# A two-layer diffusion backbone on one core: the products of V as one step per head, the order searched in ten stretches, and a pad of 32 bytes

## The chip, the cores and the metric

The kernel runs on one core of a Trainium2 chip. The core has a matrix engine, TensorE (PE in the rows; its weight loads stand apart as PEld), and three engines for everything that is not a matrix product: VectorE (DVE), ScalarE (ACT) and GpSimd (POOL). SyncE (SP) issues the transfers between HBM and the on-chip memory SBUF. TensorE writes its results into PSUM, eight banks of 128 x 512 numbers. The metric is the device time of one execution in microseconds; the times of a kernel are given as the median of three runs.

## The reference: what is computed

512 latent tokens `x` and 256 context tokens `ctx`, each of 1024 features, pass two layers. Each layer is a token mixer and a squared-ReLU MLP, both behind an RMS norm and a modulation (shift, scale, gate) made from a conditioning vector. Layer 0 mixes by neighbourhood attention with 16 heads of 64 features; layer 1 mixes by sliding-window attention with 4 heads of K and V for 16 of Q, a sink logit and rotary positions. Latent queries attend in one softmax to their local latent keys and to all context keys. Only layer 0 computes new context tokens. Cut to what matters:

```python
for i in range(DEPTH):                       # DEPTH = 2
    u_lat = modulate(rms_norm(h_lat, g_mix[i]), sh1, sc1)
    u_ctx = modulate(rms_norm(h_ctx, g_mix[i]), csh1, csc1)
    if i % 2 == 0:
        q, k, v = split(u @ na_wqkv)         # latent and context, q and k normed
        y_lat = neighborhood_attention(ql, kl, vl, kc, vc, na_rpb) @ na_wo
        y_ctx = context_attention(qc, kc, vc) @ na_wo
    else:
        y_lat = sliding_window_attention(rope(ql), rope(kl), vl, kc, vc, swa_sink) @ swa_wo
    h_lat = h_lat + ga1 * y_lat
    h_lat = h_lat + ga2 * (square(relu(modulate(rms_norm(h_lat)) @ mlp_w1[i])) @ mlp_w2[i])
    # layer 0 does the same for h_ctx with y_ctx
# one head and one block of queries:
s = concat(q @ k_local.T * scale + bias, q @ k_ctx.T * scale)
p = softmax(s)
o = p[local] @ v_local + p[ctx] @ v_ctx
```

All of it is in 32-bit floats.

## The kernel before, in words

**Products.** The large products (projections, scores, MLP) take each operand as a sum of two rounded parts (type fp32r), so one product is three on TensorE. The transposes of the attention weights and the products of V take plain 32-bit floats. One such product is one instruction of the program, and the trace shows it as two rows.

**Attention of a head.** `attn0(p, i)` is one head of layer 0, `Head1` one of layer 1. The scores of four blocks of 128 latent queries (and, in layer 0, of the context queries) come out of TensorE, VectorE adds bias or mask, ScalarE takes the exponential, and the result is scaled. TensorE then transposes these weights piece by piece into PSUM banks of the pool `p_pt`. `evac_pt` copies four (or three) transposed blocks at a time from PSUM into one slot of `PTr`, on ScalarE or VectorE. These slots lie in the region tile R.

**The products of V.** V of a head has 64 columns, half the width of TensorE. `mm_halves` issues two products that use the left and the right half (`tile_position` (0, 0) and (0, 64)) and write to the upper and the lower half of one PSUM bank, `po`. In the rows of the trace these products are called `128*64`. Layer 0 has four such steps for each head: the two blocks of context keys (512 columns each), two pairs of local blocks (192 and 256 columns), and last the context's own queries (256 columns). Layer 1 has three: 512, 256 and 384 columns. `merge` then adds the two halves of the bank: one copy of one half into `otmp` and one add on VectorE.

**What sets the order.** The code records every operation as a `Step` with its reads and writes; `together()` makes one step of several instructions of TensorE. A planner (`Plan`) then gives each step a cost by a table of its own and decides, engine by engine, which step stands next. The order of an engine is fixed by this before the kernel runs. Some steps may go to either of two engines, and the planner chooses. `Plan.search` tries many orders: it starts from the order of the code, moves steps that TensorE waited for forward (`hurry`), shakes the ranking by random amounts (`shaken`) and keeps the best. It does so in two stretches. The first ends at `cut`, in the middle of the MLP of layer 0; the second takes the rest. Since every operation is issued by one line of `build`, nearly all rows of the trace have the same line, L542, and are told apart by their tiles.

**Memory.** RA (rounded parts) and FA (floats) are two large tiles, then come small constants (`ident`, the identity for the transposes, `perm`, `ones`, `cst` and others), and behind them the region tile R, which is used for four things in turn: a ring of loads, V and `PTr` in layer 0, weights in the MLPs, and V and `PTr` again in layer 1. The eight PSUM banks are called pq.

**Stages.** By the profile: loading and the first norms from 0 to 40 us, the first projections up to 80 us, attention of layer 0 from 80 to 425 us with the projections of the next heads woven in, its output projection up to 470 us, the MLP of layer 0 up to 1000 us, keys and values of layer 1 up to 1082 us, its attention up to 1225 us, and the rest up to 1617.7 us.

Of the kernel before, what the change touches and what calls it, by code (L numbers as in the profile page):

```python
# [118 lines left out]
class Plan:  # L119
# [98 lines left out]
    def cost(self, x):  # L218
        if x.eng == "PE":
# [16 lines left out]
            else:  # L236
# [7 lines left out]
                x.occ = sum(2 * (m / 1.2 + (47 if cols == 64 else 3)) for m in runs)  # L244
# [219 lines left out]
    def search(self, rounds, tries, cut):  # L464
# [7 lines left out]
        rnd = random.Random(1)  # L472

        def of(rank, first, upto):
            s = self.forward(rank, first.copy(), upto)
            s.rank, s.last = rank, s.start[cut] if upto else max(s.end)
            return s

        def rounds_of(rank, first, upto, n, least=200):
            best = None  # L480
            for k in range(n):
# [3 lines left out]
                rank = self.hurry(rank if s.last < best.last * 1.004 else best.rank, s, least)  # L485
            return best

        first, rank = self.begin(), [float(x.i) for x in self.steps]
        for upto in (cut, None):
            found = [rounds_of(rank, first, upto, 3 * rounds)]  # L490
            for k in range(tries):
                found.sort(key=lambda s: s.last)
                found.append(rounds_of(self.shaken(found[k % 2].rank, rnd), first, upto, rounds, rnd.choice((100, 200))))
            first = best = min(found, key=lambda s: s.last)
        s = best
# [24 lines left out]
def build(nc, tc, a):  # L520

    with ExitStack() as es:
        plan, regions, cut = _build(nc, tc, a, es)
# [12 lines left out]
        for step in plan.search(ROUNDS, TRIES, cut):  # L536
# [9 lines left out]
ROUNDS, TRIES = 10, 24  # L546
# [9 lines left out]
def _build(nc, tc, a, es):  # L556
# [76 lines left out]

    (RX,) = region((F32, 4096))
# [297 lines left out]
    def bias_tables():  # L932

        for c in range(16):
# [3 lines left out]
            yield  # L938

# [171 lines left out]
    def attn0(p, i):  # L1111
# [61 lines left out]
        mm_halves(blocks, start=True)  # L1173
# [7 lines left out]
        mm_halves([(po[:, 0:192], Vs(0), pt[:, 0:192]), (po[:, 64:320], Vs(1), pt[:, 192:448])])  # L1181
# [7 lines left out]
        mm_halves([(po[:, 192:448], Vs(2), pt[:, 0:256]), (po[:, 320:512], Vs(3), pt[:, 256:448])], stop=True)  # L1189
        merge(OT_lat[:, p], po, i)  # L1190
# [208 lines left out]
    for p in range(7):  # L1399
# [5 lines left out]
        else:  # L1405
            run(ad)
            p_mm = Banks(4, 5)
            weave(at, (qkv0(p + 1), 7))
# [581 lines left out]
```

## Time and profile before

| what | before |
|---|---|
| median of 3 runs | 1621.09 us (1620.41 to 1621.33) |
| the profiled execution | 1619.86 us |
| its span (first to last instruction) | 1617.7 us |
| instructions in the span | 24693 |
| TensorE busy | 1596.9 us, 99% |
| VectorE, ScalarE, GpSimd busy | 1174.1, 814.0, 248.3 us |
| granted clock of TensorE, mean | 0.999 |

Times in the rows below are microseconds from the start of the span, unless a column says otherwise. A row of the timeline gives the start, the length, the engine, the operation, what it writes and reads, its shape, and how many instructions of the kind follow each other (x4); in brackets stands how long the engine was idle before it, and what ended the wait. Successive products overlap in the array, so the length of a row runs past the start of the next one: the time that a row takes from its engine is read from start to start. Some records of products are missing in a trace, so a count in such a row can be a little low.

### The profile page before, as it was taken

What the parts mean: (1) busy time and instruction counts of PE and PEld (TensorE: products, weight loads), DVE (VectorE), ACT (ScalarE), POOL (GpSimd) and SP (SyncE); (2) the same over time, 40 slices, a digit from 0 to 9 for tenths busy, and PEclk for the clock granted to TensorE, in tenths of its full rate; (3) what the DMA queues carried; (4) which work ended last, traced back from release to release, by engine and by line L of the source; (5) the groups of instructions that cost most, each with busy time, mean ns of one, the idle gap of its engine ahead of it and who ended that gap; (6) DMA issues with size and microseconds to landing.
All of it is one profiled execution on the core that took longest, in us unless ns stands there. A gap on an engine that the chain in (4) does not pass through costs nothing.

```text
span 1617.7 us, 24693 instructions
## 1 busy us (share of the span) xinstructions
PE 1596.9 (99%) x9356; PEld 1332.1 (82%) x9356; DVE 1174.1 (73%) x2376; ACT 814.0 (50%) x1627; POOL 248.3 (15%) x220
## 2 busy tenths in 40 slices
PE   8999999999999999999999999999999999999999
PEld 4788888887888888888888888787768888888887
DVE  4798777887488676676786767999996855556554
ACT  4687667776355242434442523677894533222220
POOL 0111111111123020312230211342200000000000
PEclk9999999999999999999999999999999999999999
DMA  9643343123324232333341422010024332222301
GB/s 347 198 134 98 116 128 99 49 65 118 102 78 147 91 129 92 119 117 129 120 141 54 142 92 78 24 43 27 20 73 163 105 105 91 102 94 79 104 27 52
DMA packets 57400, 165.59 MB, mean 102 GB/s; under 512 B 6593, under 2 KB 16193, under 8 KB 57153
## 3 DMA queue, kind: packets, MB, share of 16 engines
q1 hardware_dynamic: 57280, 164.01, 31.0%
q8 instruction: 73, 1.20, 0.3%
q14 instruction: 47, 0.38, 0.1%
HBM read 159.79 MB, written 7.34 MB: 103 GB/s over the span
## 4 chain that ended last, share of the span: by engine, by line
PE 92%; DVE 5%; ACT 2%; issue 1%; DMA 1%; POOL 0%; SPq 0%; DVEq 0%; ACTq 0%; POOLq 0%
PE pq L542 92%; DVE FA L542 2%; DVE RA L542 2%; DVE smalls L542 1%; ACT FA L542 1%; ACT RA L542 0%; ACT R L542 0%; DMA FA<-in_wqkv_dram 0%; DMA FA<-in_xT_dram 0%; POOL FA L542 0%; ACT smalls L542 0%; DVE R L542 0%; SPq L542 0%; DVEq L542 0%; DVE amod L542 0%
## 5 line engine op out<-in xcount | busy, mean ns | idle before, releaser
L542 PE MATMUL pq<-RA 128*128 128x512 f32 (+3 forms) x6560 | 1274.6, 348 | 6.9 <-ACT RA L542 2.8
L542 PEld LDWEIGHTS pq<-RA 128*128 128x128 f32 x6560 | 1053.5, 189 | 166.5 <-issue 14.5
L542 ACT CAST RA<-FA 128x1024 fp32r<-128x1024 f32 (+3 forms) x283 | 225.9, 812 | 347.6 <-PE pq L542 260.8
L542 DVE SCALAR_TENSOR_TENSOR FA<-pq,mods,FA 128x512 f32<-128x512 f32 (+1 forms) x413 | 263.5, 661 | 132.9 <-PE pq L542 131.6
L542 DVE TENSOR_TENSOR RA<-FA,RA 128x1024 fp32r<-128x1024 f32 (+3 forms) x248 | 244.4, 997 | 98.1 <-ACT RA L542 96.7
L542 PE MATMUL pq<-RA,R 128*128 128x512 f32 (+1 forms) x870 | 182.3, 352 | 0.0
L542 PEld LDWEIGHTS pq<-RA,R 128*128 128x128 f32 x870 | 143.7, 188 | 25.4 <-issue 0.8
L542 ACT ACTIVATE FA<-FA,smalls 128x512 f32<-128x512 f32 (+1 forms) x166 | 121.4, 741 | 26.8 <-DVE smalls L542 26.2
L542 POOL TENSOR_TENSOR RA<-FA,RA 128x512 fp32r<-128x512 f32 (+1 forms) x35 | 51.0, 1457 | 539.8 <-ACT RA L542 539.2
L542 PE MATMUL pq<-ident,FA 128*128 128x128 f32 x800 | 129.8, 276 | 3.2 <-DVE FA L542 1.9
L542 PEld LDWEIGHTS pq<-ident,FA 128*128 128x128 f32 x800 | 94.8, 140 | 26.4 <-issue 6.9
L542 DVE TENSOR_TENSOR R<-R,FA 128x1024 f32<-128x1024 f32 x84 | 103.8, 1260 | 15.0 <-ACT FA L542 7.8
L542 POOL TENSOR_SCALAR FA<-FA,s 128x1024 f32<-128x1024 f32 x24 | 78.4, 3265 | 221.7 <-DMA FA<-in_ada_w_dram 179.0
L542 POOL TENSOR_TENSOR FA<-FA,smalls 128x256 f32<-128x256 f32 (+2 forms) x81 | 59.8, 743 | 341.4 <-DVE smalls L542 249.3
L542 ACT ACTIVATE FA<-FA,s 128x1024 f32<-128x1024 f32 x60 | 68.9, 1151 | 69.5 <-POOL FA L542 54.0
L542 ACT ACTIVATE FA<-pq 128x512 f32<-128x512 f32 (+1 forms) x96 | 49.9, 522 | 82.6 <-PE pq L542 82.6
L542 DVE SCALAR_TENSOR_TENSOR FA<-pq,FA 128x512 f32<-128x512 f32 (+1 forms) x96 | 57.0, 596 | 45.4 <-ACT FA L542 45.2
L542 ACT ACTIVATE FA<-FA 128x256 f32<-128x256 f32 (+1 forms) x130 | 58.9, 455 | 47.7 <-DVE FA L542 42.7
L542 ACT COPY R<-pq 128x512 f32<-128x512 f32 (+4 forms) x145 | 68.6, 491 | 28.2 <-PE pq L542 25.7
L542 PE MATMUL pq<-R 128*64 128x512 f32 (+2 forms) x448 | 79.2, 463 | 0.7 <-DVE FA L542 0.7
L542 POOL TENSOR_TENSOR FA<-FA 128x256 f32<-128x256 f32 (+2 forms) x59 | 47.4, 816 | 191.5 <-ACT FA L542 130.5
L542 ACT COPY FA<-pq 128x256 f32<-128x256 f32 (+4 forms) x98 | 42.4, 433 | 57.1 <-PE pq L542 54.2
(84 smaller groups left out, 994.7 us busy)
## 6 DMA issues: line engine op xcount, KB each, us to landing
FA<-in_w_dram SPq DMA_DIRECT2D x128, 512.0 KB, 3.5
FA<-in_ada_w_dram SPq DMA_DIRECT2D x80, 512.0 KB, 3.8
FA<-in_wqkv_dram SPq DMA_DIRECT2D x24, 384.0 KB, 3.3
FA<-in_wo_dram SPq DMA_DIRECT2D x16, 512.0 KB, 3.4
FA<-in_ada_dram SPq DMA_DIRECT2D x10, 512.0 KB, 10.3
FA<-in_wq_dram SPq DMA_DIRECT2D x8, 512.0 KB, 3.5
R<-in_ada_dram SPq DMA_DIRECT2D x6, 512.0 KB, 10.9
FA<-in_xT_dram SPq DMA_DIRECT2D x4, 512.0 KB, 6.7
```

Of the source, the lines that this page charges most:

```text
L542: tc.keep_in_program_order(getattr(e, f)(*map(real, args), **{k: real(x) for k, x in kw.items()}))
```

## The change

Three things are changed, and two smaller ones go with them.

First, `mm_halves` takes all products of V of a head at once and makes one step of them. In layer 0 that joins the four steps of a head (the product for the context's queries included, which now writes to a bank of `p_pt` instead of the bank of V), in layer 1 the three steps. The planner's cost for such a step is adapted by one term.

Second, `search` takes a list of marks instead of the one `cut`. There are ten marks: after the heads p = 0, 2, 4 and 6 of layer 0, after the output projection, in the middle of the MLP, after the keys and values of layer 1, and after each of the first three groups of heads of layer 1. Each stretch is searched with a look ahead to the next mark, by the time that TensorE spends without work; the numbers of rounds and tries are 8 and 16 instead of 10 and 24.

Third, a constant of 128 x 8 floats (32 bytes in each partition) is placed between FA and the constants, so that the region tile begins at a multiple of 128 bytes.

In layer 1 `PTr` has five slots instead of three, one of them in FA; for this the mask is cut from 896 to 640 columns, and the rotary tables move.

```diff
-                x.occ = sum(2 * (m / 1.2 + (47 if cols == 64 else 3)) for m in runs)
+                x.occ = sum(2 * (m / 1.2 + (47 if cols == 64 else 3)) for m in runs) - (38 * (len(runs) - 1) if cols == 64 else 0)
...
-            s.rank, s.last = rank, s.start[cut] if upto else max(s.end)
+            s.rank, s.last = rank, (max(s.free[pe], s.start[upto]) if upto else max(s.end)) - s.done
...
-                rank = self.hurry(rank if s.last < best.last * 1.004 else best.rank, s, least)
+                rank = self.hurry(rank if s.last < best.last + 4000 else best.rank, s, least)
...
-        first, rank = self.begin(), [float(x.i) for x in self.steps]
-        for upto in (cut, None):
-            found = [rounds_of(rank, first, upto, 3 * rounds)]
+        source = [float(x.i) for x in self.steps]
+        first, rank, marks = self.begin(), source, cuts + [None]
+        for q, mark in enumerate(marks):
+            far = marks[min(q + 1, len(marks) - 1)]
+            found = [rounds_of(r, first, far, 2 * rounds) for r in ((rank, source) if q else (source,))]
             for k in range(tries):
                 found.sort(key=lambda s: s.last)
-                found.append(rounds_of(self.shaken(found[k % 2].rank, rnd), first, upto, rounds, rnd.choice((100, 200))))
-            first = best = min(found, key=lambda s: s.last)
+                found.append(rounds_of(self.shaken(found[k % 2].rank, rnd), first, far, rounds, rnd.choice((100, 200))))
+            best = min(found, key=lambda s: s.last)
+            rank = best.rank
+            if mark:
+                first = of(rank, first, mark)
...
-ROUNDS, TRIES = 10, 24
+ROUNDS, TRIES = 8, 16
...
+    const("pad", [128, 8])
     (RX,) = region((F32, 4096))
...
-    def mm_halves(pairs, start=False, stop=False):
+    def mm_halves(*sums):
 
         with together():
-            for at, (out, st, mv) in zip((0, 64), pairs):
-                pe.matmul(out[at : at + 64], st, mv, start=start, stop=stop, tile_position=(0, at))
+            for pairs in sums:
+                for n, pair in enumerate(pairs):
+                    for at, (out, st, mv) in zip((0, 64), pair):
+                        pe.matmul(out[at : at + 64], st, mv, start=n == 0, stop=n == len(pairs) - 1, tile_position=(0, at))
...
-        mm_halves(blocks, start=True)
+        pairs = [blocks]
...
-        mm_halves([(po[:, 0:192], Vs(0), pt[:, 0:192]), (po[:, 64:320], Vs(1), pt[:, 192:448])])
+        pairs.append([(po[:, 0:192], Vs(0), pt[:, 0:192]), (po[:, 64:320], Vs(1), pt[:, 192:448])])
...
-        mm_halves([(po[:, 192:448], Vs(2), pt[:, 0:256]), (po[:, 320:512], Vs(3), pt[:, 256:448])], stop=True)
-        merge(OT_lat[:, p], po, i)
+        pairs.append([(po[:, 192:448], Vs(2), pt[:, 0:256]), (po[:, 320:512], Vs(3), pt[:, 256:448])])
...
-        po = p_pv.next()[:, 0:256]
-        mm_halves([(po, Vs(4 + c), pt[:, c * 256 : c * 256 + 256]) for c in range(2)], start=True, stop=True)
-        merge(OT_ctx[:, p], po, i)
+        pc = p_pt.next()[:, 0:256]
+
+        mm_halves(pairs, [[(pc, Vs(4 + c), pt[:, c * 256 : c * 256 + 256]) for c in range(2)]])
+        merge(OT_lat[:, p], po, i)
+        merge(OT_ctx[:, p], pc, i)
...
-    mask = FA[:, 4096:4992]
-    rope = FA[:, 4992:6016].rearrange("p (e t d) -> p e t d", e=4, t=4)
+    mask = FA[:, 4096:4736]
+    rope = FA[:, 5120:6144].rearrange("p (e t d) -> p e t d", e=4, t=4)
...
-    PTr = Slots(*(RX[:, 2176 + 512 * i : 2688 + 512 * i] for i in range(3)))
+    PTr = Slots(*(RX[:, 2176 + 512 * i : 2688 + 512 * i] for i in range(3)), RX[:, 3712:4096], FA[:, 4736:5120])
...
             ee = ends()
-            mm_halves(blocks, start=True)
             yield
-            blocks = [mid(1)]
-            mm_halves(ee)
+            mids = [mid(1)]
             yield
-            blocks.append(mid(2))
-            yield
-            mm_halves(blocks, stop=True)
+            mids.append(mid(2))
+            mm_halves([blocks, ee, mids])
             merge(OT_lat[:, h // 2], po, h % 2)
```

The order of the instructions shows what becomes of the steps. The first place is TensorE at the last heads of layer 0. In these rows pq7 is the bank of V, R00 the region tile, `ident` the identity, and 64x512 a product of V of 512 columns. Before:

```order
L542 MATMUL pq7_72<-R00_124 64x256 x2
L542 MATMUL pq2_67<-ident_73,FA_64 128x128
L542 MATMUL pq3_68<-ident_73,FA_64 128x128 x3
L542 MATMUL pq2_67<-ident_73,FA_64 128x128
L542 MATMUL pq5_70<-RA_63 128x512 x5
L542 MATMUL pq2_67<-ident_73,FA_64 128x128 x2
L542 MATMUL pq7_72<-R00_124 64x512 x2
L542 MATMUL pq7_72<-R00_124 64x192
L542 MATMUL pq7_72<-R00_124 64x256 x2
L542 MATMUL pq7_72<-R00_124 64x192
L542 MATMUL pq4_69<-RA_63 128x512 x2
L542 MATMUL pq5_70<-RA_63 128x512
```

Here the three latent steps of a head already stand behind each other, while the context's product (the row at the top, of the head before) stands alone. In the order of the change, the same stage:

```order
L547 MATMUL pq2_68<-ident_74,FA_64 128x128 x7
L547 MATMUL pq7_73<-R00_125 64x512 x2
L547 MATMUL pq7_73<-R00_125 64x192
L547 MATMUL pq7_73<-R00_125 64x256 x2
L547 MATMUL pq7_73<-R00_125 64x192
L547 MATMUL pq6_72<-R00_125 64x256 x2
L547 MATMUL pq0_66<-RA_63 128x256 x4
L547 MATMUL pq1_67<-RA_63 128x512 x2
```

The context's product has moved up to the end of the latent ones and writes to pq6, a bank of `p_pt`. The second place is TensorE at a head in the middle of the attention of layer 1, before:

```order
L542 MATMUL pq3_68<-ident_73,FA_64 128x128
L542 MATMUL pq7_72<-R20_8853 64x512 x2
L542 MATMUL pq2_67<-RA_63 128x128 x2
L542 MATMUL pq1_66<-RA_63 128x512
L542 MATMUL pq0_65<-RA_63 128x512 x2
L542 MATMUL pq1_66<-RA_63 128x512
L542 MATMUL pq7_72<-R20_8853 64x256 x2
L542 MATMUL pq3_68<-ident_73,FA_64 128x128 x4
L542 MATMUL pq7_72<-R20_8853 64x384 x2
```

and in the order of the change, at a late head of the same layer:

```order
L547 MATMUL pq6_72<-ident_74,FA_64 128x128 x3
L547 MATMUL pq0_66<-RA_63 128x512 x6
L547 MATMUL pq4_70<-RA_63 128x512
L547 MATMUL pq7_73<-R20_8852 64x512 x2
L547 MATMUL pq7_73<-R20_8852 64x256 x2
L547 MATMUL pq7_73<-R20_8852 64x384
L547 MATMUL pq7_73<-FA_64,R20_8852 64x384
L547 MATMUL pq4_70<-RA_63 128x512 x2
```

Scores (RA, 128x512) and transposes no longer stand between the three pieces; the last piece reads its slot from FA.

## Rows read from the trace of the kernel before

**Rows 1.** The page: busy time of the engines, and the chain that ended last.

```profile
PE 1596.9 (99%) x9356; PEld 1332.1 (82%) x9356; DVE 1174.1 (73%) x2376; ACT 814.0 (50%) x1627; POOL 248.3 (15%) x220
...
PE 92%; DVE 5%; ACT 2%; issue 1%; DMA 1%; POOL 0%; SPq 0%; DVEq 0%; ACTq 0%; POOLq 0%
```

**Rows 2.** Windows: length, busy PE, PEld, DVE, ACT, POOL, granted clock, DMA share, GB/s.

```profile
80.00:425.00 345.00, 342.30 (x2284) 290.61 (x2285) 272.73 (x804) 244.63 (x648) 48.86 (x65) 1.00 0.32 101
...
1082.00:1225.00 143.00, 141.90 (x907) 100.81 (x906) 129.88 (x368) 126.33 (x283) 24.16 (x31) 1.00 0.16 54
```

**Rows 3.** Waits of PE: us in total, times, longest; of seven rows.

```profile
PE pq L542 <- DVE R L542: 5.9, 1, 5.9
...
PE pq L542 <- ACT RA L542: 2.8, 3, 1.8
...
PE pq L542 <- DVE smalls L542: 0.5, 2, 0.3
```

**Rows 4.** Timeline of PE at the longest waits behind the loading phase.

```profile
80.75 4.10 PE L542 MATMUL pq<-RA 128*128 128x256 f32 x28 [1.55 <-ACT FA L542]
...
1028.63 7.08 PE L542 MATMUL pq<-RA 128*128 128x512 f32 x28 [0.92 <-DVE RA L542]
1036.80 0.66 PE L542 MATMUL pq<-ident,FA 128*128 128x128 f32 x4 [1.09 <-DVE FA L542]
```

**Rows 5.** Timeline of PE: the first and the last of 69 groups.

```profile
91.70 1.84 PE L542 MATMUL pq<-R 128*64 128x512 f32 x12
...
1222.85 0.87 PE L542 MATMUL pq<-R 128*64 128x384 f32 x4
```

**Rows 6.** Timeline of PE, layer 1, a joined group and the next.

```profile
1094.37 1.51 PE L542 MATMUL pq<-R 128*64 128x512 f32 x8
1095.81 0.88 PE L542 MATMUL pq<-ident,FA 128*128 128x128 f32 x6
1096.62 0.87 PE L542 MATMUL pq<-R 128*64 128x384 f32 x4
1097.41 0.77 PE L542 MATMUL pq<-ident,FA 128*128 128x128 f32 x5
```

**Rows 7.** Timeline of PE, layer 1, a head whose steps stand apart.

```profile
1174.18 1.08 PE L542 MATMUL pq<-R 128*64 128x512 f32 x4
1175.19 1.41 PE L542 MATMUL pq<-RA 128*128 128x128 f32 x6
1176.53 0.65 PE L542 MATMUL pq<-R 128*64 128x256 f32 x4
1177.11 0.66 PE L542 MATMUL pq<-ident,FA 128*128 128x128 f32 x4
```

**Rows 8.** Timeline of PE: undisturbed products and transposes.

```profile
453.43 2.32 PE L542 MATMUL pq<-RA 128*128 128x256 f32 x18
455.59 0.86 PE L542 MATMUL pq<-RA,R 128*128 128x256 f32 x6
...
1196.06 1.15 PE L542 MATMUL pq<-ident,FA 128*128 128x128 f32 x9
```

**Rows 9.** Timeline of PE, layer 0, the last heads.

```profile
407.93 1.81 PE L542 MATMUL pq<-RA 128*128 128x256 f32 x13
409.67 1.84 PE L542 MATMUL pq<-R 128*64 128x512 f32 x12
411.44 7.08 PE L542 MATMUL pq<-RA 128*128 128x256 f32 x46
```

**Rows 10.** Groups by form: count, busy us, mean ns of one, idle before.

```profile
L542 PE MATMUL pq<-ident,FA 128*128 128x128 f32 x800 | 129.8, 276 | 3.2 <-DVE FA L542 1.9 <-ACT R L542 0.8 <-DVE RA L542 0.3
L542 ACT COPY R<-pq 128x512 f32<-128x512 f32 x74 | 41.7, 587 | 15.3 <-PE pq L542 14.4
L542 DVE COPY R<-pq 128x512 f32<-128x512 f32 x22 | 15.1, 687 | 6.6 <-PE pq L542 6.5
L542 PE MATMUL pq<-ident,R 128*128 128x128 f32 x40 | 10.4, 277 | 0.0
```

More of the change, by code (lines that the diff above doesn't have):

```diff
@@ L462, in shaken, with search @@
         return [r + shift.setdefault(i // size, rnd.gauss(0.0, span)) for i, r in enumerate(rank)]
-    def search(self, rounds, tries, cut):
+    def search(self, rounds, tries, cuts):
         self.epochs()
@@ L471, in search @@
                 self.steps[j].succ.append(x.i)
-        rnd = random.Random(1)
+        rnd, pe = random.Random(1), self.ALL.index("PE")
         def of(rank, first, upto):
             s = self.forward(rank, first.copy(), upto)
-            s.rank, s.last = rank, s.start[cut] if upto else max(s.end)
+            s.rank, s.last = rank, (max(s.free[pe], s.start[upto]) if upto else max(s.end)) - s.done
             return s
@@ L522, in build @@
     with ExitStack() as es:
-        plan, regions, cut = _build(nc, tc, a, es)
+        plan, regions, cuts = _build(nc, tc, a, es)
         tiles, now, open_ = {}, -1, ExitStack()
@@ L534, in turn @@
                 tiles[k, j] = pool.tile([128, n], dtype, name=f"R{k}{j}", tag="R")
-        for step in plan.search(ROUNDS, TRIES, cut):
+        for step in plan.search(ROUNDS, TRIES, cuts):
             while step.epoch is not None and now < step.epoch:
@@ L938, in bias_tables, with mark @@
             yield
+    cuts = []
+    def mark():
+        cuts.append(next(x.i for x in reversed(plan.steps) if x.eng == "PE"))
     raw, raw0 = Ring(FA, FX, 768, 2), Ring(FA, FX, 1024, 2)
@@ L1408, in _build @@
             weave(at, (qkv0(p + 1), 7))
+        if p in (0, 2, 4, 6):
+            mark()
     wo0.take(0, Stream(Ring(FA, FX, 1024, 2), [(a["wo0"][0, q], u) for q, u in enumerate((wx, wslots[2], wslots[0], wslots[3]))], 4))
@@ L1417, in _build @@
     split_o(7)
-    cut = []
     def mlp(layer, T_ctx, stream, tmp, side, st_lat, st_ctx, between=None, after_ctx=None):
@@ L1545, in mlp @@
             if c == NCH // 2 and T_ctx:
-                cut.append(next(x.i for x in reversed(plan.steps) if x.eng == "PE"))
+                mark()
             if c + 1 < NCH:
@@ L1597, in _build @@
     wo0.rest(stream, Banks(0,1,7,2,3), *st, lambda: mod_lat(0, 1, tmp2))
+    mark()
     def between():
@@ L1795, in front @@
                     scores(ps, T1, T2, q0, with_context(K, 0))
-                    mk = mask[:, 0:768].rearrange("p (s n) -> p s n", s=2)[:, :, 0:256]
+                    mk = FA[:, 4096:4864].rearrange("p (s n) -> p s n", s=2)[:, :, 0:256]
                     col[t] = {0: 256, 1: 384, 4: 0, 5: 128}
@@ L1874, in _build @@
     kv1()
+    mark()
     heads = [Head1(h) for h in range(16)]
@@ L1896, in _build @@
             weave((go(), 24 if gr else 21), (q1(gr + 1), 8))
+            mark()
         else:
@@ L1919, in _build @@
     mlp(1, False, stream, Ring(FA, FX + 5120, 512, 5), iter(()), None, None, between=lambda: half_done(256))
-    return plan, regions, cut[0]
+    return plan, regions, cuts
 def layout(inputs):
```

## The prediction, written before the changed kernel was run

> **What bounds the kernel now.** I read the page first. TensorE (PE) is busy 99% of the span of 1617.7 us, and the chain that ended last lies on it for 92% [rows 1]. The reader is to see that work taken off another engine gains nothing: time comes only from what TensorE itself spends. A busy PE is not a PE at its pace, though, so I went on to the stages. In the attention of layer 0 (80 to 425 us) and of layer 1 (1082 to 1225 us) PE is busy 342.30 of 345 and 141.90 of 143 us, at a granted clock of 1.00, the upper of its two levels (2.4 GHz) [rows 2]. The list of what PE waited for gives the real holes: seven rows that sum to 16.5 us, 5.9 us of them the first product's wait for its first input, and 1.8 us the longest of three waits for ScalarE's first results [rows 3]. The largest of the others are 1.55 us where the attention of layer 0 begins and 0.92 and 1.09 us at the hand-over between the layers [rows 4]. So waiting that another order could fill is about 16.5 - 5.9 - 1.8 = 8.8 us; whatever else can be won is hidden inside "busy".
>
> It is hidden where TensorE changes between products of full width and the products of V, which are 64 wide (128*64 in the rows). A group of 64-wide products is one row of TensorE's timeline. Between the first at 91.70 us and the last at 1222.85 us there are 69 of them, 34 in layer 0 and 35 in layer 1 [rows 5]; the order of the program before has the same 69.
>
> **What a group costs beyond its columns.** The old order already puts some of a head's steps back to back, which gives a price without an experiment. Inside: in layer 1 a joined group (512 columns, then 256; 8 rows of the trace) takes from its start to the start of what follows 1095.81 - 1094.37 = 1.44 us [rows 6]; the same two pieces apart take 1175.19 - 1174.18 = 1.01 and 1177.11 - 1176.53 = 0.58 us [rows 7]. Joining them saves 1.59 - 1.44 = 0.15 us. Outside: between two groups stand six transposes that take 1096.62 - 1095.81 = 0.81 us [rows 6]. A row of nine transposes lasts 1.15 us; less the 0.28 us that one of them lasts [rows 10], that is 0.87 us for eight steps, 0.11 us each [rows 8]. Six should take 0.66, so the change out of 64 wide and back in costs 0.15 us. Between full-width products: 13 of 256 columns stand between two groups and take 409.67 - 407.93 = 1.74 us [rows 9]; at a pace of (455.59 - 453.43) / 18 = 0.120 us [rows 8] they should take 1.56, so there the change costs 0.18 us. A group that is joined to another thus saves 0.15 + 0.15 = 0.30 us where transposes stand behind it, and 0.15 + 0.18 = 0.33 us where full-width products do.
>
> The rows give this change a price, 0.30 to 0.33 us, and not its cause. The Trainium skill has one: "Changing tiling mode (not just tile) drains the TensorE" (TensorEngine Tiling (Array Packing), Key Properties). With the drain of roughly 175 ns that its page TensorE: Matmul & The Clock Gate states (Single matmul latency), once on the way in and once on the way out, my estimate by these pages would be 0.35 us for each group, and 13.0 us for the 37 counted next.
>
> **The change part by part.** (1) The steps of V joined. In the new order each of the 32 heads has one group: 32 instead of 69, so 37 fewer. In the old order 38 groups are followed by full-width products, 28 by transposes and 3 by 32-wide products; in the new one 17, 12 and 3. So 21 x 0.33 + 16 x 0.30 = **11.7 us** are saved, with bounds 11.1 (all at 0.30) and 12.2 (all at 0.33). The products themselves, their columns, the transposes and the copies are as many in both orders. The 32-wide groups (modulation vectors) rise from 34 to 36; at the same price that is 0.6 us **lost** (bounds 0 and 0.7).
>
> (2) What the join makes wait. All products of a head now stand behind its last copy out of PSUM, and all five copies keep their slots until then. Behind a group that waits, everything of TensorE is queued. The last copy takes ScalarE 587 ns or VectorE 687 ns [rows 10]. In layer 0 only the last pair of products needs it, and the pairs ahead of it take 411.44 - 409.67 = 1.77 us [rows 9]; in layer 1 the 384-column pairs at the end need it, and 1.44 us of others stand ahead [rows 6]. So even transposes put right before the group leave the copy covered: I take **nothing**. Without that cover (the copy late, because its engine has other work ahead of it) a head loses up to one copy, so the bounds are 0 and 32 x 0.69 = 22 us. I stay at the near end because 19 of the 32 groups have, at the paces above, over 1 us of other products between the last transpose before them and themselves. The transposing bank that the context products now take, and the two added slots in layer 1, go with this item. The merge of the latent half into the output (one ScalarE copy, one VectorE add) comes some 0.4 us later; its reader, the split for the output projection, is many us off.
>
> (3) The order searched in ten stretches. It moves instructions on every engine, SP's loads among them; the loads stand in one order through the first 30, and the first products nearly so, so the loading phase (0 to 40 us) stays. It can win from the 8.8 us above, and marks lie at both places with the large holes (within the attention of layer 0, and behind the keys and values of layer 1). I take 2.5 us **gained**: the two holes at the hand-over and a third of the one at 80 us. The upper bound is all 8.8. A new order can also lose; for that I allow 3 us, about as much as it is to win.
>
> (4) The pad. 32 bytes move the identity and everything behind it, and put the region tile R on a multiple of 128 bytes, so R began 96 bytes past one; RA and FA stand before the pad. Does an operand there run slower? A transpose that reads its data from R lasts 277 ns, from FA 276 [rows 10]. That is 0.4%, and a row of transposes steps at 0.11 us whatever each lasts. I take **nothing**; at 1 ns for each of the 40 from R, and for each copy into it, the bounds are within 0.5 us to both sides.
>
> Sum for the profiled execution: 1617.7 - 11.7 + 0.6 - 2.5 = 1604.1 us of span. That execution took 1619.86 us, 1.2 less than the median of 1621.09. Taken from the median: 1621.1 - 13.6 = **1607.5 us**.
>
> **The rivals.** A, the forecast: 1603 to 1611 (search between 7 us gained and 1 lost, the rest as summed): 0.64.
>
> B, half of the gain goes into new waits: the copies sit behind other work, and TensorE stands in front of a group or inside it. For it: a head's five copies now come due together, and VectorE is busy 129.88 of 143 us in the attention of layer 1 [rows 2]. Against it: both engines have the same copies as before, and TensorE has other products between them. At 0.19 us a head it costs 6 us: 1613.5. The skill says of array packing that it speeds up TensorE and not the emptying of PSUM (TensorEngine Tiling (Array Packing), PSUM Bottleneck); no row above shows TensorE held by that. Range 1611 to 1617.8: 0.17.
>
> C, the search fills nearly all of the holes: 8 us instead of 2.5, so 1602; range 1598 to 1603: 0.12.
>
> D, no change beyond what can be measured (0.2%, 3.2 us, is about what a measurement of this kernel can tell from none): the groups go, but TensorE then waits for what it was going to wait for anyway, with VectorE as the bound. 1618 to 1624: 0.03. Then the holes of rows 3 should be larger already.
>
> E, slower: the pad moves the identity, the moving operand of the transposes, by 32 bytes, off the multiple of 128 on which RA and FA suggest it stood. If that slows a transpose, 840 of them (800 from FA, 40 from R) [rows 10] stand on TensorE's own path. From 13.6 / 840 = 16 ns each (0.11 us becomes 0.126) the gain is gone, from 20 ns the kernel is slower by over 0.2%, and at 25 ns it ends at 1607.5 + 21 = 1628.5. Against it: R stood off such a multiple, and transposes of its data show nothing. But no row has the identity there: 0.04.
>
> **How the numbers follow.** Faster by over 0.2% are A, B and C: 0.93; within it D, 0.03; slower E, 0.04. The range runs from the middle of C to the middle of B, 1600.5 to 1614.5: outside lie about 0.05 of C, 0.07 of B and the 0.07 of D and E, 0.19 in all.
>
> **What would show it.** Joins: 32 rows of 64-wide groups in TensorE's timeline, in layer 0 of 1.77 + 0.58 - 0.15 = 2.20 us to the next start, in layer 1 of 1.44 + 0.79 - 0.15 = 2.08 us (0.79 is 1097.41 - 1096.62, rows 6). If they are longer, the copies are late (B). The two attention stages should shrink by 18 x 0.32 = 5.8 and 19 x 0.32 = 6.1 us, the MLPs by nothing. Search: the list of PE's waits falls below 16.5 us, above all at the hand-over; if it rises, (3) has the wrong sign. Pad: transposes in a row keep their 0.11 us. The prediction is wrong altogether if the time of a change of width only moves into the next wait; then the stages keep their length although 37 groups are gone.

## The result, and the profile after

| what | before | after |
|---|---|---|
| median | 1620.75 us (1619.78 to 1621.33, 4 runs) | 1603.0 us (1602.22 to 1604.23, 4 runs) |
| ratio | | 0.9893, 95% interval 0.9877 to 0.9909 |
| span of the profiled execution | 1617.7 us | 1602.5 us |
| instructions in the span | 24693 | 24687 |

The change wins 17.7 us (14.7 to 19.9 by the interval of the ratio), where 13.6 were forecast. The page of the changed kernel, the lines that answer to [rows 1]:

```profile
PE 1584.2 (99%) x9356; PEld 1337.8 (83%) x9356; DVE 1178.7 (74%) x2385; ACT 810.5 (51%) x1624; POOL 235.9 (15%) x214
...
PE 93%; DVE 4%; ACT 2%; issue 1%; DMA 0%; POOL 0%; DVEq 0%; SPq 0%; ACTq 0%
```

TensorE is as full as before, with the same 9356 rows of products, and spends 12.7 us less on them. Of the 15.2 us by which the span shrank, 12.7 are busy time: most of what was saved was hidden inside "busy". The windows of [rows 2] after the change, with the same columns:

```profile
80.00:425.00 345.00, 341.81 (x2321) 296.85 (x2320) 279.90 (x816) 248.39 (x656) 56.91 (x70) 1.00 0.33 108
1082.00:1225.00 143.00, 141.57 (x910) 106.39 (x909) 133.42 (x352) 124.01 (x272) 28.31 (x33) 1.00 0.20 68
```

In the first window as much of the time is busy as before, but 2321 products fit in it instead of 2284; VectorE is at 133.42 of 143 us in the second and still hardly holds TensorE up: of PE's waits only 0.2 us in that window are for VectorE. The waits of PE over the whole span (in total, times, longest), the four largest of eight rows:

```profile
PE pq L547 <- DVE R L547: 6.3, 2, 6.1
PE pq L547 <- ACT RA L547: 2.7, 3, 2.1
PE pq L547 <- DVE RA L547: 1.5, 2, 1.2
PE pq L547 <- DVE smalls L547: 1.0, 1, 1.0
```

All eight sum to 13.6 us, against 16.5 in [rows 3]. Without the first product's wait and the longest one for ScalarE's first results, which are the loading phase, 13.6 - 6.1 - 2.1 = 5.4 us are left of the 8.8 that another order could fill. The holes that answer to [rows 4] are smaller, 1.16 us instead of 1.55 where the attention of layer 0 begins, and 0.69 and 0.18 instead of 0.92 and 1.09 at the hand-over:

```profile
82.79 5.45 PE L547 MATMUL pq<-RA 128*128 128x512 f32 x38 [1.16 <-DVE RA L547]
...
1029.17 0.66 PE L547 MATMUL pq<-ident,FA 128*128 128x128 f32 x4 [0.69 <-DVE FA L547]
...
1030.48 0.63 PE L547 MATMUL pq<-ident,FA 128*128 128x128 f32 x4 [0.18 <-ACT RA L547]
```

In the timeline of PE stand a group of layer 0 and what follows it, a group of layer 1 and what follows it, and nine transposes (in layer 1 some slots lie in FA, so one group is printed as several rows):

```profile
158.01 2.27 PE L547 MATMUL pq<-R 128*64 128x512 f32 x16
160.21 1.07 PE L547 MATMUL pq<-FA,s 128*32 128x256 f32 x16
...
1073.75 1.83 PE L547 MATMUL pq<-R 128*64 128x512 f32 x9
...
1075.84 1.19 PE L547 MATMUL pq<-RA 128*128 128x128 f32 x5
...
1197.74 1.14 PE L547 MATMUL pq<-ident,FA 128*128 128x128 f32 x9
```

From start to next start the groups take 160.21 - 158.01 = 2.20 us and 1075.84 - 1073.75 = 2.09 us; 2.20 and 2.08 were forecast. There are 32 of them: all 16 of layer 0 take 2.20, and 15 of layer 1 take 2.09 (one takes 2.14). The transposes step by (1.14 - 0.28) / 8 = 0.11 us, as before.

Where the time came from is read at rows that mark the same place of the program in both kernels: the first product that sums the squares of a norm (with `ones`) behind the attention of layer 0, at the start of layer 1, and before the last MLP. Before:

```profile
450.32 1.03 PE L542 MATMUL pq<-FA,ones 128*128 128x512 f32 x2
...
1014.49 1.02 PE L542 MATMUL pq<-FA,ones 128*128 128x512 f32 x2
...
1264.21 0.70 PE L542 MATMUL pq<-FA,ones 128*128 128x256 f32 x2 [0.34 <-DVE FA L542]
```

After:

```profile
445.01 1.07 PE L547 MATMUL pq<-FA,ones 128*128 128x512 f32 x2
...
1008.93 1.13 PE L547 MATMUL pq<-FA,ones 128*128 128x512 f32 x2
...
1250.17 0.70 PE L547 MATMUL pq<-FA,ones 128*128 128x256 f32 x2
```

Up to the first mark 5.3 us are won; from there to the second 0.3; from the second to the third, with the keys, values and attention of layer 1, 249.7 - 241.2 = 8.5; in the rest (1617.7 - 1264.2 against 1602.5 - 1250.2) 1.2. Products may stand on the other side of a mark in the new order, so these are good to about 1 us. The shape is that of the forecast (5.8 and 6.1 for the two attentions, the hand-over's holes beside them), except for the last 1.2 us: that stretch has no products of V. The second experiment shows where they come from.

### The profile page after: what moved, and what is told of

Its sections match the earlier page's. It is cut to its first block, busy times and chain, and to the rows that moved or that the text cites. A ratio compares the mean times of both kernels' runs of the same rounds, so it can differ in the third digit from the quotient of the medians.

```text
span 1602.5 us, 24687 instructions
## 1 busy us (share of the span) xinstructions
PE 1584.2 (99%) x9356; PEld 1337.8 (83%) x9356; DVE 1178.7 (74%) x2385; ACT 810.5 (51%) x1624; POOL 235.9 (15%) x214
## 4 chain that ended last, share of the span: by engine, by line
PE 93%; DVE 4%; ACT 2%; issue 1%; DMA 0%; POOL 0%; DVEq 0%; SPq 0%; ACTq 0%
PE pq L547 93%; DVE FA L547 2%; DVE RA L547 2%; ACT FA L547 1%; ACT RA L547 1%; DVE smalls L547 0%; DMA FA<-in_xT_dram 0%; DMA FA<-in_cT_dram 0%; DVE R L547 0%; ACT R L547 0%; ACT smalls L547 0%; POOL FA L547 0%; SPq L547 0%; DVEq L2003 0%; DVEq L547 0%
## 5 line engine op out<-in xcount | busy, mean ns | idle before, releaser
L547 DVE TENSOR_TENSOR RA<-FA,RA 128x1024 fp32r<-128x1024 f32 (+3 forms) x251 | 248.6, 1001 | 98.1 <-ACT RA L547 95.4
L547 PE MATMUL pq<-ident,FA 128*128 128x128 f32 x800 | 125.0, 275 | 2.4 <-ACT R L547 0.7
L547 POOL TENSOR_TENSOR RA<-FA,RA 128x512 fp32r<-128x512 f32 (+1 forms) x32 | 45.3, 1416 | 506.7 <-ACT RA L547 466.9
L547 POOL TENSOR_TENSOR FA<-FA,smalls 128x256 f32<-128x256 f32 (+2 forms) x79 | 63.6, 809 | 336.4 <-DVE smalls L547 253.7
L547 POOL TENSOR_SCALAR FA<-FA,s 128x1024 f32<-128x1024 f32 x24 | 75.0, 3126 | 198.2 <-DMA FA<-in_ada_w_dram 106.3
L547 ACT COPY FA<-pq 128x256 f32<-128x256 f32 (+5 forms) x111 | 47.6, 429 | 74.0 <-PE pq L547 59.9
L547 POOL TENSOR_TENSOR FA<-FA 128x256 f32<-128x256 f32 (+2 forms) x58 | 43.9, 771 | 230.6 <-ACT FA L547 191.1
L547 ACT COPY R<-pq 128x512 f32<-128x512 f32 (+4 forms) x130 | 62.4, 504 | 23.1 <-PE pq L547 22.1
L547 PE MATMUL pq<-R 128*64 128x256 f32 (+3 forms) x416 | 70.7, 452 | 0.0
```

The costliest lines, as they stand in the source:

```text
L547: tc.keep_in_program_order(getattr(e, f)(*map(real, args), **{k: real(x) for k, x in kw.items()}))
```

## The experiments

**1. Each part by itself.** Four kernels, timed beside 21 runs of before (median 1620.97): the pad alone (the order is that of before), the joins alone with the old search in two stretches, the new search alone without joins, and the whole change without the pad (the order is that of after).

```diff
 e1:  before  +    const("pad", [128, 8])
 e2:  after   -    const("pad", [128, 8])
              -    def search(self, rounds, tries, cuts):
              +    def search(self, rounds, tries, cut):      # the search of before, 10 rounds, 24 tries
 e3:  before  +    def search(self, rounds, tries, cuts):     # the search of after, its ten marks, 8 rounds, 16 tries
 e4:  after   -    const("pad", [128, 8])
```

> The kernel before with the 32-byte pad alone; its order of instructions is unchanged. Theory P (weights that stand in R slow a product while R lies off a multiple of 128 bytes): in the traces of before and after, a product of 512 columns with weights from R steps at 233.3 ns before and 227.5 ns after, one of 256 columns at 117.5 and 119.6 ns. 546 x -5.8 ns and 324 x +2.1 ns give 2.5 us less, a span of about 1615.2 us, all of it in the two MLPs and the projections. Rival N (the pad does nothing, as my prediction took it, and the pace of the MLPs fell because of the new order): within 0.5 us of before, and products from R keep 233 ns. Rival E (the moved identity slows the transposes): over 1 us longer, transposes above 109 ns each.

> The steps of V joined (with the cost term and the slots of layer 1), searched in the old two stretches, without the pad. Its order has 32 groups of 64-wide products and 34 of 32-wide ones. Theory J (each of the 37 groups that go was worth 0.30 to 0.33 us): 11.1 to 12.2 us less than before, with the old search's luck 2 us to either side: 1607 to 1611 us. Rival W (the joins turn into waits): less than 6 us gained, and the groups are longer than 2.20 and 2.09 us or PE's list of waits grows by several us.

> The search in ten stretches alone, on the steps of before, without the pad. Its order has 65 groups of 64-wide and 31 of 32-wide products, 4 and 3 fewer than before, which is worth 2.1 us at 0.3 us each. Theory S (the search is worth what joins and pad leave, 17.75 - 11.7 - 2.5 = 3.5 us and more): 3 to 6 us less than before, and PE's waits fall below 16.5 us. Rival L (it is luck of one order, worth nothing by itself): within 2 us of before.

> The changed kernel without the pad, in the same order of instructions. Theory P: 2.5 us more than the changed kernel, about 1605.5 us, and products with weights from R step at 233 ns again. Rival N: the same as the changed kernel within 0.5 us.

| run | us | ratio, 95% interval | PE waits, sum of the list |
|---|---|---|---|
| the pad alone | 1618.13 | 0.9983 (0.9974 to 0.9992) | 16.7 |
| the joins alone | 1615.13 | 0.9961 (0.9948 to 0.9974) | 20.0 |
| the search alone | 1620.31 | 0.9994 (0.9985 to 1.0003) | 18.5 |
| joins and search, no pad | 1606.63 | 0.9911 (0.9897 to 0.9924) | 13.6 |

The pad is worth 2.8 us by itself (1.3 to 4.2 by the interval), and 2.9 on top of the rest (0.9911 against 0.9893, whose intervals overlap). The search alone wins nothing that can be told from none, and its list of waits is longer than before. The joins alone win 5.8 us. Together, without the pad, they win 14.3. So the two do not add up: 7.8 us come only when both are there.

The traces say what is won and lost. All steps of PE into, inside and out of the 64-wide and 32-wide groups were summed, from start to next start, less the undisturbed pace of the full-width products and transposes among them and less the listed waits. This sum is 10.1 us smaller than before with joins and search, 9.9 with the joins alone, and still 3.3 with the search alone, whose order has 65 groups instead of 69. It is good to about 0.6 us: by so much the pad alone, in the order of before, differs from before.

The joins alone lose 3.5 us of this to longer waits (20.0 against 16.5) and 1.8 to pauses that are too short for the list: 9.9 - 3.5 - 1.8 = 4.6, against 1617.7 - 1613.3 = 4.4 us between the two profiled executions. The search alone loses all of its 3.3 us and more in its profiled execution: 2.0 to longer waits, 1.8 to a slower clock, the rest to short pauses. The clock shows behind a wait of 2.31 us for GpSimd that ends at 462.42 us: nine products of 512 columns take about 420 instead of 227 ns, and the granted clock from 462 to 467 us is 0.66. So rival W held for the joins alone, by its waits (of their groups only one, of 2.64 us, is longer than it should be), and rival L for the search alone.

What the joins lose in waits under the old search is seen in the list of PE's waits of that run (three of nine rows) and in its timeline, with the waits in brackets:

```profile
PE pq L542 <- POOL FA L542: 3.0, 2, 1.7
PE pq L542 <- ACT RA L542: 2.8, 3, 1.3
PE pq L542 <- DVE smalls L542: 2.7, 5, 1.0
```

```profile
467.17 0.70 PE L542 MATMUL pq<-FA,ones 128*128 128x256 f32 x2 [1.71 <-POOL FA L542]
...
1261.03 0.70 PE L542 MATMUL pq<-FA,ones 128*128 128x256 f32 x2 [1.32 <-POOL FA L542]
...
1263.81 0.39 PE L542 MATMUL pq<-RA,R 128*128 128x256 f32 x1 [1.25 <-ACT RA L542]
```

The largest of the new waits do not stand at the groups. They stand where a norm is passed from one stage to the next, and PE waits for GpSimd's and ScalarE's part of it. At the norm of 1261.03 the kernel of before has 0.34 us and the changed kernel nothing (the rows of the norms above). That the products which could fill such a pause are used up earlier when the groups are shorter is argued, not shown.

**2. Where the pad's gain lies.** The durations that my step (4) went by show little. The groups by form (count, busy us, mean ns of one, idle before), products whose stationary operand lies in R, before the change:

```profile
L542 PE MATMUL pq<-RA,R 128*128 128x512 f32 x546 | 138.1, 395 | 0.0
L542 PE MATMUL pq<-RA,R 128*128 128x256 f32 x324 | 46.2, 281 | 0.0
```

and after it:

```profile
L547 PE MATMUL pq<-RA,R 128*128 128x512 f32 x546 | 136.1, 391 | 0.0
L547 PE MATMUL pq<-RA,R 128*128 128x256 f32 x324 | 47.3, 285 | 0.0
```

The pace from start to start shows it. In the MLP of layer 1, a row of such products and the start of the next row; before:

```profile
1405.29 11.13 PE L542 MATMUL pq<-RA,R 128*128 128x512 f32 x47
1416.26 0.40 PE L542 MATMUL pq<-RA 128*128 128x512 f32 x1
```

After:

```profile
1393.38 8.55 PE L547 MATMUL pq<-RA,R 128*128 128x512 f32 x37
1401.76 18.55 PE L547 MATMUL pq<-RA 128*128 128x512 f32 x81
```

(1416.26 - 1405.29) / 47 = 0.2334 us before, (1401.76 - 1393.38) / 37 = 0.2265 after; products of that MLP with both operands in RA step at 0.227 in both kernels. The pad alone, in the order of before, has the same 47 products:

```profile
1405.68 10.81 PE L542 MATMUL pq<-RA,R 128*128 128x512 f32 x47
1416.34 0.39 PE L542 MATMUL pq<-RA 128*128 128x512 f32 x1
```

(1416.34 - 1405.68) / 47 = 0.2268 us. From the first mark above to the last product, where the order is the same, the steps of products with their stationary operand in R take 2.4 us less with the pad alone than before (2.9 less at 512 columns, 0.5 more at 256), and all other steps 0.3 less; with the pad on top of the rest it is 2.2 and 0.5 less. Behind the third mark, where there are no products of V, the pad alone wins 2.3 us (1617.7 - 1264.2 against 1616.4 - 1265.2), more than the 1.2 us that the whole change wins there.

To see what the pace depends on, three more kernels keep the order of after and move the tiles only. Counted from the start of RA by the sizes of the tiles, RA and FA begin at a multiple of 128 bytes in before and after; R begins 96 bytes past one before, and on one after.

```diff
 e7:  the pad stands in front of RA instead of in front of the constants: RA, FA at 32, R at 0
 e8:  +    const("shift", [128, 16])     # in front of RA, the pad kept: RA, FA, R at 64
 e9:  -    const("pad", [128, 8])
      +    const("pad", [128, 24])       # RA, FA at 0, R at 64
```

> The changed kernel in its own order with the pad of 32 bytes in front of RA and FA instead of behind them: R and all constants stay where the change puts them, RA and FA stand 32 bytes past a multiple of 128. Theory P (weights off a multiple of 128 bytes slow a product of 512 columns by 5.9 ns, and make one of 256 columns 2 ns faster): 3272 x 5.9 = 19 us more, 2360 x 2 = 5 us less, and 864 of 384 columns anywhere from 2 us less to 5 us more: 12 to 20 us slower than the changed kernel, and products from RA at 233 ns. Rival Q (something about R alone, its place behind the other tiles): products from RA keep 227 ns, the time within 1 us of the changed kernel.

> The changed kernel in its own order with 64 bytes more in front of RA: RA, FA and R all stand 64 bytes past a multiple of 128, the identity 96. Theory P with 128 bytes as the grain: as the run before and R's products besides, 14 to 23 us slower. Theory P with 64 bytes as the grain: within 1 us of the changed kernel, products at 227 ns.

> Pad of 96 bytes instead of 32: R begins 64 bytes past a multiple of 128, RA and FA on one; the order is that of the changed kernel. Theory 64 (weights in R and a moving operand in RA must agree to 64 bytes): start-to-start pace of the 512-column products with weights in R stays at 227 ns, time as the changed kernel, ratio near 0.989. Theory 128 (they must agree to 128 bytes): the pace is 233 ns, as without the pad, and the time 2.5 to 3 us longer, ratio near 0.991.

The same row in the kernels with RA at 32 and R at 0, with all three at 64, and with R at 64 alone:

```profile
1393.36 8.80 PE L547 MATMUL pq<-RA,R 128*128 128x512 f32 x37
1401.99 18.30 PE L547 MATMUL pq<-RA 128*128 128x512 f32 x80
```

```profile
1394.55 8.55 PE L547 MATMUL pq<-RA,R 128*128 128x512 f32 x37
1402.94 17.41 PE L547 MATMUL pq<-RA 128*128 128x512 f32 x76
```

```profile
1394.02 8.80 PE L547 MATMUL pq<-RA,R 128*128 128x512 f32 x37
1402.65 17.65 PE L547 MATMUL pq<-RA 128*128 128x512 f32 x77
```

These take 8.63, 8.39 and 8.63 us for 37 products: 233, 227 and 233 ns. Over all pairs of neighbouring products of one shape with the stationary operand in R, behind 470 us (some 455 pairs of 512 columns, 255 of 256; steps in which the engine paused, over 250 and 130 ns, are left out), start to start:

| start of R against RA, modulo 128 bytes | kernels | 512 columns | 256 columns | us, ratio |
|---|---|---|---|---|
| 96 | before | 233.2 ns | 117.4 ns | |
| 96 | no pad | 233.2 | 117.4 | 1606.63, 0.9911 |
| 96 | RA 32, R 0 | 233.3 | 117.5 | 1605.96, 0.9901 (0.9886 to 0.9916) |
| 64 | RA 0, R 64 | 233.3 | 115.4 | 1605.35, 0.9901 (0.9885 to 0.9916) |
| 0 | pad alone | 227.3 | 119.6 | 1618.13, 0.9983 |
| 0 | after | 227.7 | 119.6 | 1603.0, 0.9893 |
| 0 | all at 64 | 227.6 | 119.6 | 1603.43, 0.9886 (0.9872 to 0.9901) |

R at 0 with RA at 32 is slow, R at 64 with RA at 64 is fast. So theory P falls as I had written it down, the place of an operand by itself: products from RA kept 227 ns with RA at 32 and at 64, and the 12 to 23 us of loss did not come. Rival Q, something about R alone, falls too, since R went back to 233 ns without being moved. What is left is the distance of R from RA, where the other operand of the product lies. A distance of 64 bytes is as slow as one of 96 for 512 columns, so the theory of 64 falls and that of 128 stands. For 256 columns the sign is the other way. The price: 546 products by 5.5 ns is 3.0 us won, 324 by 2.2 ns 0.7 us lost, 2.3 us in sum, against 2.8 and 2.9 measured. The times of the kernels with RA at 32, with R at 64, of after and with all at 64 lie within each other's intervals; it is the pace that tells them apart. Other distances were not tried.

**3. The price of a boundary.** Is the time of a change of width really paid for each group, or would another wait take it up? A group of layer 0 (16 of the 32) is split again, by a pass of one column through the identity (full width) between the latent and the context products; in its rival the same pass stands in front of the group.

```diff
-            for f, args, kw in step.calls:
+            for n, (f, args, kw) in enumerate(step.calls):
...
+                if len(step.calls) == 8 and step.mode == 64 and n == 6:     # e6: n == 0
+                    tc.keep_in_program_order(e.matmul(plan.pc[step.i][:, 0:1], plan.ident[:], plan.ident[:, 0:1], start=True, stop=True))
```

> The changed kernel in its own order, but in each of the 16 heads of layer 0 one full-width product of a single column (the identity by its first column, into the bank of the context's products, which the next product overwrites) stands between the latent and the context's products of V. That splits 16 groups of 64-wide products in two. Theory J (a group costs 0.30 to 0.33 us beyond its columns): 16 x 0.33 = 5.3 us more than the next run, which has the same 16 products in another place. Rival M (the price only moves into a wait that comes anyway): less than 2 us between the two.

> The same 16 single-column products, but in front of the group, where TensorE works at full width or with transposes already, so that no group is split. Theory J and rival M alike: 16 products of at most 0.1 us, and a wait for the bank that comes a little earlier: 0 to 2 us more than the changed kernel.

The split kernel took 1608.65 us (1608.0 to 1609.0; ratio 0.9916, 0.9901 to 0.9931), its rival 1605.48 (1604.7 to 1605.8; 0.9897, 0.9881 to 0.9914); spans 1606.2 and 1602.9. The intervals of the ratios overlap, but not the executions: 3.2 us lie between the medians. The timeline of PE at one group, split:

```profile
156.55 0.49 PE L549 MATMUL pq<-ident,FA 128*128 128x128 f32 x3
156.97 1.84 PE L549 MATMUL pq<-R 128*64 128x512 f32 x12
158.74 0.38 PE L548 MATMUL pq<-ident 128*128 128x1 f32 x2
159.05 0.65 PE L549 MATMUL pq<-R 128*64 128x256 f32 x4
159.63 1.07 PE L549 MATMUL pq<-FA,s 128*32 128x256 f32 x16
```

and with the pass in front:

```profile
156.73 0.49 PE L549 MATMUL pq<-ident,FA 128*128 128x128 f32 x3
157.05 0.28 PE L548 MATMUL pq<-ident 128*128 128x1 f32 x2
157.26 2.27 PE L549 MATMUL pq<-R 128*64 128x512 f32 x16
159.46 1.07 PE L549 MATMUL pq<-FA,s 128*32 128x256 f32 x16
```

From the first of the three transposes to the 32-wide products: 159.63 - 156.55 = 3.08 against 159.46 - 156.73 = 2.73 us, so 0.35 us for a boundary at this place. Over the 3.2 us it would be 0.20 for each of the 16, but the places are not alike. Six rows of products to either side, the split kernel takes 0.34 to 0.36 us more than its rival at ten of the 16 groups and 0.09 to 0.15 at five; at four of these five, 32-wide products stand in front of the group, so that the rival's pass makes a boundary of its own. At one group the two are equal, because a wait for VectorE behind it is shorter by as much (0.5 against 0.9 us). The sum is 4.2 us, and from the first of these groups to the end the profiled executions differ by as much (1606.2 - 96.3 against 1602.9 - 97.0, that is 4.0 us); the 0.7 us between this and the spans lie ahead of all groups. So a boundary is paid where it stands, about 0.35 us beside full-width work, and its price moved into a wait at one of 16 places. My 0.30 to 0.33 was a little low, and my 5.3 us for the pair took the rival to be free.

By the Trainium skill a change of tiling mode "drains the TensorE" (TensorEngine Tiling (Array Packing), Key Properties). The trace fits: the boundary here costs 0.35 us, and the products that it separates are the same in both kernels. That a drain is the cause no run here shows.

**4. One lucky order?** The gain of the joins could hang on the one order that the search found. Two kernels start the random numbers of the search from 2 instead of 1: the joins alone under the old search, and the changed kernel. A third corrects the planner, whose cost of a joined group is 0.04 to 0.2 us above the 2.20 and 2.09 us of the trace, and searches longer.

```diff
 e10, e11:
-        rnd = random.Random(1)
+        rnd = random.Random(2)
 e12:
-                x.occ = sum(2 * (m / 1.2 + (47 if cols == 64 else 3)) for m in runs) - (38 * (len(runs) - 1) if cols == 64 else 0)
+                x.occ = sum(m for *_, m in kinds) / 1.2 + 168 if cols == 64 else sum(2 * (m / 1.2 + 3) for m in runs)
-ROUNDS, TRIES = 8, 16
+ROUNDS, TRIES = 12, 32
```

> The joins alone under the old search, as in the run of the joins alone (-5.8 us), with another start of its random numbers. Theory S (the old search with two stretches cannot place the longer groups): again at most 7 us gained, PE waits near 20 us in the list. Theory L (one unlucky order): the gain moves by 3 us or more, towards 10 to 12 us, and the list of waits falls to 16 us or less.

> The changed kernel with another start of the random numbers in its search. Theory S (ten stretches find an order with few waits whatever the start): within 2 us of the changed kernel, waits of 12 to 15.5 us. Theory L (the changed kernel's order is a lucky one): 3 us or more slower than the changed kernel, waits of 17 us or more.

> A try for a faster version: the planner's cost of a joined group is set to what the trace of the changed kernel shows (its columns at 1.2 a ns plus 168 ns, where the planner has 0.04 to 0.2 us more), and the search gets 12 rounds and 32 tries instead of 8 and 16. If the planner's error and the short search leave waits behind, 1 to 4 us less than the changed kernel, with waits of 10 to 12 us; if the waits left are those of the data's own order, the same within 1 us.

| run (before: 1621.2) | us | ratio, 95% interval | PE waits, sum of the list |
|---|---|---|---|
| joins alone, other start | 1619.01 (1614.34 to 1621.62) | 0.9986 (0.9977 to 0.9995) | 19.9 |
| after, other start | 1605.51 | 0.9904 (0.9891 to 0.9918) | 15.5 |
| after, corrected cost, longer search | 1606.00 | 0.9905 (0.9892 to 0.9919) | 13.9 |

The joins under the old search won 5.8 and 2.2 us, with 20.0 and 19.9 us of waits; with the new search three orders won 17.7, 15.7 and 15.2, with 13.6, 15.5 and 13.9. Less the 2.8 us of the pad, which only the second set has, it is 5.8 and 2.2 against 14.9, 12.9 and 12.4. The sets stay far apart, so this is no luck of one order; within a set the order is worth about 3 us. The search alone was run from one start only. The changed kernel with the other start lies 1.8 us behind by the ratios, within the 2 us of theory S, its waits at the upper end of what that theory allowed. The hole at the norm can come back in the new search too: the changed kernel with the other start waits 2.19 us for GpSimd there, at 1252.78 us. The third kernel is not faster but 1.9 us slower by the ratios, which neither of its two theories had: an exact cost and a longer search found nothing, and no kernel of this study is faster than the changed one by more than the noise.

The 19.9 us of the first row are not its whole loss. At the same two places as above its timeline has

```profile
1262.04 0.70 PE L542 MATMUL pq<-FA,ones 128*128 128x256 f32 x2 [1.34 <-POOL FA L542]
1262.39 1.18 PE L542 MATMUL pq<-RA 128*128 128x256 f32 x7
1264.82 0.58 PE L542 MATMUL pq<-RA,R 128*128 128x256 f32 x1 [1.25 <-ACT RA L542]
...
1267.12 0.84 PE L542 MATMUL pq<-RA,R 128*128 128x256 f32 x3
1267.76 0.84 PE L542 MATMUL pq<-RA 128*128 128x256 f32 x3
```

and the window of it (columns as in [rows 2])

```profile
1260.00:1280.00 20.00, 17.41 (x93) 15.59 (x93) 12.55 (x23) 9.81 (x18) 4.14 (x2) 0.83 0.31 110
```

Behind the two holes a product of 256 columns takes (1267.76 - 1267.12) / 3 = 0.21 us instead of 0.12: TensorE ran at the lower of its two levels until about 1270 us, and the granted clock of the window is 0.83. That cost about 2.6 us (19 products of 256 columns at 0.21 instead of 0.12 us and four of 512 at about 0.42 instead of 0.23), which no list of waits shows. The first kernel with the joins alone has the same two holes and a clock of 1.00 in this window, so the holes alone do not decide it. It is not the only such stretch: between 80 and 87 us, where PE waits 0.94 us for a DMA and then 0.67 us for VectorE, the granted clock is 0.54 (1.00 in the first kernel with the joins alone), which costs about 2 us more. Over its eleven executions the mean clock of this kernel lies between 0.993 and 0.998, and the three at 0.997 or 0.998 took 1614.3, 1617.0 and 1617.7 us. So a part of the gap between 5.8 and 2.2 us is clock and not waits. In the profiled execution the steps at the groups take 11.6 us less than before; 3.4 us of waits, the 4.6 of clock and about 3 of short pauses leave 0.5 (1617.7 against 1617.2).

## Why the prediction was right, and where it was not

The time, 1603.0 us, lies within the range and 4.5 us below the 1607.5 that I named; the side was right. It stands on the border of the forecast's own 1603 to 1611, and the pad, which the sum had at nothing, is most of the difference.

- **Step (1), the joins: right.** The groups number 32 and last what they should (2.20 and 2.09 us). Joins and search without the pad win 14.3 us; 2.9 of it are shorter waits (16.5 to 13.6), which leaves 11.4 for the joins with the 32-wide groups, against 11.7 - 0.6 = 11.1. That is a difference of two numbers; the sum over the steps at the groups, which is a measurement of its own, gives 10.1 in the kernel without the pad. The split gave 0.35 us for a boundary beside full-width work.
- **Step (2), no new waits: right for this kernel, and only with its search.** The copies out of PSUM cost nothing, as the length of the groups shows. But under the old search the joins bring 3.5 us of waits (20.0 against 16.5), at places that the step did not look at: where the attention ends and a norm has to be passed. Rival B foresaw new waits in front of the groups; they were neither there nor left in the changed kernel.
- **Step (3), the search: its size right, its meaning wrong.** The waits fell by 2.9 us, 2.5 were forecast. I had put that down to the search as a gain over the old order. Over the old order it wins nothing (0.7 us, the interval reaches over 1): what its fewer groups save goes into waits and clock. Its worth is that it lets the joins keep their gain: without it 5.8 and 2.2 us are won, with it 14.3. Why the old search does so badly with the longer steps was not tried; the new one has more stretches, another measure of an order and more tries in all, and none of these was taken by itself.
- **Step (4), the pad: the step that failed.** Taken at nothing, with bounds of 0.5 us; measured 2.8 and 2.9 us, of which the products with their stationary operand in R show 2.2 to 2.4 in the traces. I looked at how long transposes and copies of R's data last, and not at the products whose stationary operand lies in R, and I read durations where only the pace from start to start tells. The Trainium skill warns of that: the end of a product in the trace is an estimate and not a measurement (Perfetto Trace Analysis, Tensor Engine Instruction (MATMUL, LD_WEIGHTS)). Here the trace agrees: the mean duration fell by 4 ns, the pace by 5.5.
- **The rivals.** C named 1602, near the 1603.0, for the wrong reason: of the 8.8 us of holes 5.4 remain, and 2.8 us came from the pad. D falls with the busy time (12.7 us less). E falls: the identity moved to 32 bytes past a multiple of 128, and the transposes kept 0.11 us.

What stays open: why the old search cannot place the longer steps; why the clock falls behind some waits and not behind others of the same length; and why the distance of two operands sets the pace, and with opposite signs for 512 and 256 columns.

## What to carry to other kernels

Where an engine is 99% busy, price the boundaries between kinds of work from start to next start, on rows where the old order happens to have them joined: that gave the length of the new groups to 0.01 us. Steps that are merged need a new order: the same merge won 2 to 6 us under the old search and 12 to 15 under the new one, and the largest pieces of the loss stood far from the merged steps, at the next place where the engine has little to fill a pause. When a change moves a tile, look at the pace of every product that reads it together with another tile, not at the length of the rows. And a control has to be read place by place too: the pass in front of the group broke no boundary at most places and another one at four.

## What was not expected of the hardware

A product of 512 columns (fp32r) steps at 227 to 228 ns when the tiles of its stationary and its moving operand begin at the same place modulo 128 bytes, and at 233 ns at a distance of 64 or 96; with 256 columns it is 120 ns at the same place, 117 at a distance of 96 and 115 at 64. The absolute place of either made no difference (0 or 64 for the fast pace, 0 or 32 for the slow one).
